# A decoder block on one core: three of four groups of gates computed behind the attention, in seven block products per pair

## The chip, the cores and the metric

The kernel is one launch on one core of a Trainium2 chip. The core has TensorE (PE, which has a separate track PEld for the loads of its stationary operand), VectorE (DVE), ScalarE (ACT), GpSimd (POOL) and SyncE (SP). Each engine works through its own list of instructions in order. SP does no arithmetic here: it starts the DMA transfers. The metric is the device time of one execution in microseconds (us).

## The reference

One layer of a decoder, in float32, for a sequence of 2048 rows of 1024 numbers. Cut to what matters:

```python
h = rmsnorm(x, attn_norm)
z = h @ w_in                       # pool channels | q | k | v | gate_pool | gate_attn
g_pool, g_attn = sigmoid(z[gate columns] + b_gate)          # 1024 columns each
a = pool_mixer(z[pool columns], w_pool, pool_scale)         # causal means over 2, 4, 8, 16 rows, minus the row
b = swa_sink_attention(q, k, v, sinks)                      # 16 query heads, window 128, blocks of 128
x = x + (g_pool * a + g_attn * b) @ w_out
h = rmsnorm(x, ffn_norm)
up = causal_depthwise_conv(h @ w_up, conv_w, conv_b)        # 2 x 2816 columns
x = x + (silu(gate) * val) @ w_down
```

The change is about the two gates: two matrices of 1024 x 1024 that multiply the same normalised input, whose results are scaled, put through a sigmoid, and multiplied with the pooled branch and the attention branch.

## The kernel before

**High and low parts.** TensorE is fed fp32r numbers. To keep float32 accuracy each operand is split into a high part (a cast, on ACT) and a low part (the source minus the high part, on DVE), and each product is three matmuls: high with high, high with low, low with high (`mm3`, L232). `split` (L213) makes the two parts of a raw weight tile: L221 is the cast, L222 the subtraction, each in two halves of 128x512.

**Chunks and projections.** The sequence is worked off in two chunks of 1024 rows. The hidden axis of 1024 is 8 tiles of 128 (k tiles). One projection of one slab of 128 output columns for half a chunk is 8 k tiles x 3 = 24 matmuls of 128x128 by 128x512; the kernel calls it a filler when it is placed between steps of the attention. The input `hs` is a list of 8 tiles, [128, 2 parts, 1024].

**The mixer** (L1422) is the part of a chunk that the change touches. First come keys and values of the chunk, then 32 attention items: four groups of query heads, 8 blocks each. An item is `scores` (L806: 8 matmuls of 128x256, then mask, maximum and four exponentials with their sums, L843), `probabilities` (L853: four transposes on PE L857, a cast on ACT L859, a subtraction on DVE L862 and a masking on POOL L865) and `values` (L874: four matmuls L885, then L895 on ACT and L896 on DVE). They are staggered: while item i has its scores, item i-1 has its transposes and item i-2 its values. Between them stand fillers, so that TensorE has work while ACT, DVE and POOL turn scores into probabilities.

**Which fillers.** `fillers(c, i)` (L143) deals out, for group i, the two gates of the slabs of group i-1 (`ga` for the attention, `gate_attn` L910, and `pg` for the pool, `gated` L954, with `combine` L966) and the pooled projection of group i (`pu`, `pooled` L921): 12 fillers over 8 items. Group 0 has queries in place of gates. The gates of group 3 (8 fillers) follow the last item, and the last item's `probabilities` and `values` run between them. Then `out_proj` (L994) multiplies the mixed tiles with w_out, `up` does w_up, and after it comes w_down.

**Seven block products.** The up projection already multiplies by a scheme with seven block products in place of eight: the class `Up` (L1111) takes a pair of weight slabs of 128 columns, splits both along the hidden axis, and the input in 2 x 2 blocks (hidden halves by halves of the chunk). Its methods `one` to `seven` are one block product each: `product` (L1098) issues 12 matmuls (4 k tiles x 3). The weights' sums A11, A12, A22, S1 to S4 are made by `Blocks` in four steps; the input's sums T1 to T4 are made by `right_t1` to `right_t4` and split by `parted` (L981: L984 on ACT, L985 on DVE).

**What sets the order of the weights.** `Stream` follows the list of `weight_order` (L155): it loads raw tiles into three buffers (pool `rp`, 4 KB per partition) up to three pieces ahead and splits them one or two ahead. Split weights go to the pool `up_` (19 buffers, 8 KB per partition), halves of a chunk to `fp` and `mp`. In chunk 0 the split weights of the mixer are also stored to HBM (`made`, `keep_weights` L247), and chunk 1 loads them back instead of splitting again. All DMAs are issued by SP in program order; each of them also waits until the one eight places before it has landed. A transfer that has to wait for a free buffer holds up those behind it on SP.

## Time and profile before

| | |
|---|---|
| Time, median of 3 runs | 2418.05 us (2417.07 to 2420.98) |
| The profiled execution's own time | 2418.99 us |
| Its span, first to last instruction | 2417.0 us |
| Granted TensorE clock | 0.999 |
| PE busy | 2397.2 us (99%), 11252 matmuls |
| DVE busy | 1838.6 us (76%) |
| ACT busy | 1122.9 us (46%) |
| POOL busy | 156.1 us (6%) |
| DMA queues | q1 (SP): 335.72 MB, 40.8% of 16 engines' span |

The page gives busy time per engine, the span in 40 slices, the DMA queues, the chain of work that ended last, and the costliest groups of instructions by line. The span of the profiled execution is 2.0 us shorter than its time, which lies around the span. In group rows, "mean" is the duration of one instruction; a matmul's mean (390 ns) contains the pipeline's depth, so the spacing of matmuls is read from runs of them in the timeline. The timeline gives start, duration, engine, line, tiles and count of each run of instructions, and in brackets the idle time before it with what ended it.

### The profile page before, as it was taken

The numbers are of one execution on the slowest core, as the hardware profiler recorded it, in microseconds if no ns is written. First come the engines' busy times: TensorE is split into PE (matmuls) and PEld (weight loads), VectorE is DVE, ScalarE is ACT, GpSimd is POOL, SyncE is SP. The second block draws the span as 40 slices with busy tenths as digits, with TensorE's granted clock in tenths as the row PEclk, the third lists the DMA queues.
The fourth block names the chain that finished last, engine by engine and source line by source line (L and its number), as shares of the span: only waits on it lengthen the run. The fifth ranks groups of instructions, "written<-read, shape, count | busy, mean of one in ns | idle before, by whom it ended". The sixth has DMA issues, their size and how long they took to land.

```text
span 2417.0 us, 30362 instructions
## 1 busy us (share of the span) xinstructions
PE 2397.2 (99%) x11252; PEld 1995.0 (83%) x11252; DVE 1838.6 (76%) x2966; ACT 1122.9 (46%) x2151; POOL 156.1 (6%) x102
## 2 busy tenths in 40 slices
PE   9999999999999999999999999999999999999999
PEld 8878888888888888788888888888888888888887
DVE  8687788765977777799946867765478777778994
ACT  7445444444555555543523533343446445554432
POOL 1113111000000000000002221110000000000000
PEclk9999999999999999999999999999999999999999
DMA  9755354268222233644344542231642222228421
GB/s 344 245 187 171 135 183 156 101 226 283 79 81 93 97 105 105 213 169 149 113 149 126 169 161 104 65 107 56 204 166 96 90 86 79 79 70 287 139 70 52
DMA packets 139026, 337.83 MB, mean 140 GB/s; under 512 B 12288, under 2 KB 48640, under 8 KB 127872
## 3 DMA queue, kind: packets, MB, share of 16 engines
q1 hardware_dynamic: 138448, 335.72, 40.8%
q8 instruction: 88, 1.44, 0.2%
q14 instruction: 58, 0.48, 0.1%
q10 hardware_dynamic: 432, 0.19, 0.0%
HBM read 231.67 MB, written 104.20 MB: 139 GB/s over the span
## 4 chain that ended last, share of the span: by engine, by line
PE 92%; DVE 3%; DMA 2%; ACT 2%; issue 1%; POOL 0%; SPq 0%; DVEq 0%; ACTq 0%; POOLq 0%
PE f L238 33%; PE f L1103 19%; PE t L1103 10%; PE a L1103 5%; PE f L1403 4%; PE a L1403 4%; PE s L1403 4%; PE t L1403 4%; PE a L885 2%; PE s L824 2%; PE a L238 1%; PE t L857 1%; DMA F<-xT 1%; DMA R<-w_out 0%; DVE U L222 0%
## 5 line engine op out<-in xcount | busy, mean ns | idle before, releaser
L238 PE MATMUL f<-U,U 128*128 128x512 f32 (+1 forms) x3936 | 917.0, 390 | 4.3 <-ACT U L221 1.8
L238 PEld LDWEIGHTS f<-U,U 128*128 128x128 f32 x3936 | 727.4, 188 | 154.7 <-DVE U L222 4.3
L1103 PE MATMUL f<-U,U 128*128 128x512 f32 x1512 | 359.8, 390 | 1.4 <-ACT Q L1121 1.4
L1103 PEld LDWEIGHTS f<-U,U 128*128 128x128 f32 x1512 | 283.4, 188 | 61.5 <-ACT Q L1121 2.2
L1169 DVE SCALAR_TENSOR_TENSOR M<-F,vc,M 128x1024 f32<-128x1024 f32 x176 | 225.3, 1282 | 140.9 <-ACT M L1166 140.5
L1103 PE MATMUL t<-U,U 128*128 128x512 f32 x1080 | 253.5, 389 | 0.8 <-ACT Q L1121 0.8
L1103 PEld LDWEIGHTS t<-U,U 128*128 128x128 f32 x1080 | 202.6, 188 | 43.2 <-ACT Q L1121 1.2
L843 ACT ACTIVATE Q<-s,st,rq 128x128 f32<-128x128 f32 x256 | 114.0, 455 | 106.6 <-DVE st L840 104.7
L334 ACT CAST U<-R 128x1024 fp32r<-128x1024 f32 x120 | 125.4, 1053 | 62.5 <-DVE R L363 31.1
L335 DVE TENSOR_TENSOR U<-R,U 128x1024 fp32r<-128x1024 f32 x120 | 146.5, 1222 | 0.0
L1103 PE MATMUL a<-U,U 128*128 128x512 f32 x576 | 139.3, 390 | 0.0
L1103 PEld LDWEIGHTS a<-U,U 128*128 128x128 f32 x576 | 108.0, 188 | 22.4
L865 POOL TENSOR_SCALAR_AFFINE_SELECT M<-M 128x1024 fp32r<-128x1024 f32 x64 | 90.8, 1419 | 541.9 <-DVE M L862 355.0
L1103 PE MATMUL f<-U,M 128*128 128x512 f32 x504 | 121.9, 389 | 0.3 <-DVE F L1147 0.3
L1361 ACT CAST U<-U 128x1024 fp32r<-128x1024 f32 x76 | 79.0, 1050 | 85.4 <-PE s L1403 22.9
L1103 PEld LDWEIGHTS f<-U,M 128*128 128x128 f32 x504 | 94.6, 188 | 20.3 <-DVE F L1147 0.7
L1166 ACT ACTIVATE M<-F,vc 128x1024 f32<-128x1024 f32 x88 | 109.4, 1243 | 2.0 <-DVE F L1151 0.5
L1155 ACT COPY F<-f 128x512 f32<-128x512 f32 x42 | 24.7, 589 | 175.4 <-PE f L1103 175.4
L222 DVE TENSOR_TENSOR U<-R,U 128x512 fp32r<-128x512 f32 x142 | 95.1, 700 | 8.0 <-ACT U L221 7.4
L1362 DVE TENSOR_TENSOR U<-U,U 128x1024 fp32r<-128x1024 f32 x76 | 92.1, 1220 | 4.1 <-ACT U L1361 3.9
L221 ACT CAST U<-R 128x512 fp32r<-128x512 f32 x142 | 80.7, 618 | 20.7 <-PE f L238 5.0
L1361 ACT CAST F<-U 128x1024 fp32r<-128x1024 f32 x44 | 46.2, 1050 | 92.7 <-PE a L1403 62.6
(271 smaller groups left out, 3569.9 us busy)
## 6 DMA issues: line engine op xcount, KB each, us to landing
R<-w_up SPq DMA_DIRECT2D x80, 512.0 KB, 3.8
actd<-M SPq DMA_DIRECT2D x44, 512.0 KB, 2.7
U<-w_down SPq DMA_DIRECT2D x88, 256.0 KB, 5.0
U<-actd SPq DMA_DIRECT2D x88, 256.0 KB, 5.3
qd<-U SPq DMA_DIRECT2D x64, 256.0 KB, 3.7
Q<-qd SPq DMA_DIRECT2D x64, 256.0 KB, 3.9
R<-w_out SPq DMA_DIRECT2D x32, 512.0 KB, 5.4
U<-kept SPq DMA_DIRECT2D x12, 1024.0 KB, 7.3
```

The source lines that it names most:

```text
L222: low = V.tensor_sub(lo[:, t], src[:, t], hi[:, t].bitcast(F32))
L238: nc.tensor.matmul(out, a, b, start=(i == 0), stop=(i == n - 1))
L334: A.copy(t[:, 0], raw)
L335: V.tensor_sub(t[:, 1], raw, t[:, 0].bitcast(F32))
L843: A.activation(pr[:, h, :], sc[:, h, 0:P], AF.Exp, bias=nm[:, h:h + 1], scale=it["rq"][:, h:h + 1], accum_out=rs[:, h:h + 1])
L865: G.affine_select(own.rearrange("p a h q -> p (a h) q"), pa.bitcast(F32).rearrange("p a h q -> p (a h) q"), pattern=[[0, 8], [1, P]], base ...
L1103: nc.tensor.matmul(bank, a[:, x, k, :], b[k // 2][:, y, k % 2, :], start=(first and i == 0), stop=(i == 11), skip_group_check=True)
L1166: A.activation(y, u[:, 2:], AF.Identity, bias=cw[:, 3, m:m + 1], scale=cw[:, 2, m:m + 1])
L1169: V.scalar_tensor_tensor(y, u[:, j:j + T], cw[:, j, m:m + 1], y, op0=ALU.mult, op1=ALU.add)
L1361: A.copy(hi, src)
L1362: V.tensor_sub(lo, src, hi.bitcast(F32))
L1403: nc.tensor.matmul(into[m], u[:, 0, c_], v[:, 1], start=(first and j == 0), stop=(k == n - 1 and j == 2), skip_group_check=True)
```

## The change

The eight items' fillers of each group are now one per item. Group 0 has the queries and pooled slabs that it had, group 1 queries, pooled slabs and the first gates of group 0, group 2 the next of them, and group 3 the last of them with its own pooled slab. So only the gates of group 0 (slabs 6 and 7) are still fillers. The gates of groups 1 to 3 are six units, one per slab (4, 5, 2, 3, 0, 1): the pair of w_ga and w_gp of that slab is multiplied with the input by the seven block products of the class `Up`, that is by 84 matmuls of 128x512 in place of 4 x 24 = 96. They run in `gates()` behind the attention; the first two block products of unit 0 (12 matmuls each) are the fillers of the last two items.

What goes with it:

- The input becomes 8 tiles of [128, 2 parts, 2 k tiles, 512] (`Input`), which serve as B11, B21 and B22. For T1 to T4 the chunk's x is read again from HBM (four transfers of 1 MB per chunk) and scaled on ACT (`scaled_input`, eight activations of 128x1024), and DVE subtracts.
- `split_added`: for `ga`, `pg`, `pu` and the first four `q` slabs in chunk 0, and for the units' weight blocks in both chunks, the low part is made without DVE. ACT casts the source to the high part (L235), ACT writes the negative of the source, cast, that is minus the high part, into the low part's place (L236), and an accumulating DMA from POOL's queue adds the source to it there (L237, 512 KB). There are 52 of these DMAs.
- The pooled difference d is stored to HBM (`dd`), as is the attention's output of groups 0 to 2 (`tad`), and the gated mix (`xd`); they are read back where they are needed. SP issues 839 DMAs in place of 757.
- The units' weights are not kept in `made`: chunk 1 loads the raw slabs and splits them again.
- The store of the carried keys and values moves ahead of the attention.

```diff
+UNITS = [ct for i in (1, 2, 3) for ct in slabs_of(i)]
+
+
 def fillers(c, i):
 
-    g = gates_of(i - 1) if i > 0 else queries_of(0) + queries_of(1)
-    pu = pooled_of(i)
-    if i == 0:
-        pu = pu[2:]
+    q = queries_of(0) + queries_of(1)
+    g = gates_of(0)
+    pu = [pooled_of(j) for j in range(4)]
+    if i == 3:
+        out = [[f] for f in g[6:] + pu[3] + [("one", 0, 0), ("two", 0, 0)]]
+        out[4].insert(0, ("gates", 0, 0))
+        return out
     fold = [("fold", j, 0) for j in FOLDS[FOLD_FIRST:] if c == 0 and i == 0]
-    out = fold + g[:4] + pu[:2] + g[4:] + pu[2:]
+    out = fold + (q[:4] + pu[0][2:] + q[4:6], q[6:] + pu[1][:2] + g[:2] + pu[1][2:],
+                  pu[2][:2] + g[2:6] + pu[2][2:])[i]
     return [out[n * len(out) // NB:(n + 1) * len(out) // NB] for n in range(NB)]
...
-        out += [(kind, j) for kind, j, n in gates_of(3) if n == 0]
+            out += [(kind, j) for parts in fillers(c, i) for kind, j, h in parts
+                    if h == 0 and kind not in ("one", "two")]
+        out += [("gates", i) for i in range(1, len(UNITS))]
...
+    def split_added(hi, lo, src):
+
+        A.copy(hi, src)
+        A.activation(lo, src, AF.Copy, scale=-1.0)
+        G.dma_start(lo, src.bitcast(F32R), accum_op=ALU.add)
...
+            if key[0] in ("ga", "pg", "pu") or key[0] == "q" and key[1] < 4:
+                split_added(hi, lo, raw)
+            else:
+                split_weights.last = split(hi, lo, raw)
...
-            A.copy(t[:, 0], raw)
-            V.tensor_sub(t[:, 1], raw, t[:, 0].bitcast(F32))
+            if self.added:
+                split_added(t[:, 0], t[:, 1], raw)
+            else:
+                A.copy(t[:, 0], raw)
+                V.tensor_sub(t[:, 1], raw, t[:, 0].bitcast(F32))
...
+    class Gates(Up):
+
+
+        def __init__(self, c, ct, b):
+            super().__init__(c, ct, b, None)
...
+    def scaled_input(c, j):
+
+        t = up_.tile([P, 2, T], F32, "U")
+        load(t, xT[2 * j * P:(2 * j + 2) * P, c * T:(c + 1) * T]
+             .rearrange("(k p) t -> p k t", p=P))
+        for k in range(2):
+            A.activation(t[:, k], t[:, k], AF.Identity,
+                         scale=vc[:, V_AN + 2 * j + k:V_AN + 2 * j + k + 1])
+        return t
+
+    def gates(c, units, b, xg, last_probabilities, last_values):
+
+
+        def weights(f, n):
+            if f < len(units):
+                if units[f].w is None:
+                    units[f].w = stream.get("gates", f)
+                units[f].w.step(n)
+
+        u0, u1, u2 = units[:3]
+        weights(1, 1)
+        u1.one()
+        last_probabilities()
+        weights(1, 1)
+        u1.two()
+        weights(2, 1)
+        right_t1(xg, b, None)
+        u2.one("t")
+        last_values()
+        xg += [scaled_input(c, j) for j in (2, 3)]
+        u2.two()
+        t2s = right_t2(xg, b, None)
+        u0.four()
+        right_t3(xg, b)
+        u0.three()
+        weights(1, 2)
+        u1.four("a")
+        u0.five()
+        right_t4(xg, b, t2s)
+        u0.fetch()
+        u0.six()
+        u0.seven()
+        u0.value()
+        weights(2, 1)
+        u1.three()
+        u0.gate()
+        weights(2, 2)
+        u1.five()
+        n = len(units)
+        for f in range(2, n):
+            u, old = units[f], units[f - 1]
+            if f > 2:
+                u.one()
+                u.two()
+            old.fetch()
+            weights(f + 1, 1)
+            old.seven()
+            old.value()
+            weights(f + 1, 1)
+            if f < n - 1:
+                u.three()
+            else:
+                u.four()
+            weights(f + 1, 1)
+            old.six()
+            old.gate()
+            weights(f + 1, 1)
+            if f < n - 1:
+                u.four()
+            else:
+                u.three()
+            u.five()
+        ms = {j: [mixed(j, 0)] for j in (3, 2, 1)}
+        x0 = up_.tile([P, 2, 2, 512], F32R, "U")
+        old.parts(x0)
+        stream.part(stream.used + 2)
+        u.fetch()
+        u.value(N1)
+        u.seven()
+        u.value(N0)
+        u.six()
+        u.attn()
+        for c_ in (N0, N1):
+            u.combine(c_)
+            if c_ == N0:
+                u.parts(x0)
+        ms[0] = [x0]
+        return ms
...
+            if units[0].w:
+                units[0].w.step(1)
+            if i == len(items) - 2:
+                run_later(9)
+                xg = [scaled_input(c, j) for j in (0, 1)]
+        done(items[-2])
         run_later(9)
-        if c + 1 < NCH:
-            for g in range(2):
-                load(carry[g, :, 0:2], kts[g][:, :, T - P:T].bitcast(F32))
-                load(carry[g, :, 2], vs[0][:, NB - 1, g].bitcast(F32))
-        for f in rest[2:4]:
-            filler(*f, c, hs, ta, st)
-            run_later()
-        ms = [mixed(ta, j) for j in (3, 2, 1)]
-        for f in rest[4:]:
-            filler(*f, c, hs, ta, st)
-            run_later()
-        stream.part(stream.used + 2)
-        return ms + [mixed(ta, 0)]
+        return gates(c, units, b, xg, lambda: probabilities(items[-1]), lambda: done(items[-1]))
```

How the order of instructions moves, at the end of the attention of chunk 0 (chunk 1 is alike). On PE, before, the rows from the last item's transposes (tile t) to its values (tile a), with a filler of 24 matmuls (tile f, weights U_350 to U_371 being the input's tiles in before) between them:

```order
L857 MATMUL t_4643<-identr_91,Q_4503 128x128 x4
L238 MATMUL f_4655<-U_350,U_4567 128x512 x3
L238 MATMUL f_4655<-U_353,U_4567 128x512 x3
L238 MATMUL f_4655<-U_356,U_4567 128x512 x3
L238 MATMUL f_4655<-U_359,U_4567 128x512 x3
L238 MATMUL f_4655<-U_362,U_4567 128x512 x3
L238 MATMUL f_4655<-U_365,U_4567 128x512 x3
L238 MATMUL f_4655<-U_368,U_4567 128x512 x3
L238 MATMUL f_4655<-U_371,U_4567 128x512 x3
L885 MATMUL a_4682<-M_4648,U_453 128x512 x2
L885 MATMUL a_4682<-M_4651,U_454 128x512 x2
L238 MATMUL f_4708<-U_350,U_4692 128x512 x3
```

In the change, the rows from unit 0's first block product (f_4046) on. The weights' tile U_3916 is unit 0's A11 and A12; U_4150 is unit 1's.

```order
L1161 MATMUL f_4046<-U_358,U_3916 128x512 x6
L924 MATMUL a_4096<-M_4036,U_452 128x512 x2
L924 MATMUL a_4096<-M_4039,U_453 128x512 x2
L863 MATMUL s_1581<-U_450,Q_3943 128x256 x8
L896 MATMUL t_4106<-identr_91,Q_4009 128x128 x4
L1161 MATMUL a_4116<-U_363,U_3916 128x512 x6
L1161 MATMUL a_4116<-U_368,U_3916 128x512 x6
L924 MATMUL a_4136<-M_4111,U_452 128x512 x2
L924 MATMUL a_4136<-M_4114,U_453 128x512 x2
L896 MATMUL t_4170<-identr_91,Q_4086 128x128 x4
L1161 MATMUL f_4155<-U_353,U_4150 128x512 x2
L1161 MATMUL a_4185<-U_363,U_4150 128x512 x2
```

Where 24 matmuls stood between two steps of the last items there are now 12, and from the last transposes (t_4170) on 2 of unit 1's first product and 2 of its second, whose other ten each follow the last values.

On ACT, in the change, the same place: L882 are the exponentials, L898 the cast behind the transposes, L934 the output's copies, L1179 the copy of unit 0's first product, L1386 the scaling of x, L235 and L236 the two steps of the split.

```order
L934 COPY Q_4024<-a_4019 64x256
L1179 COPY Q_4059<-f_4046 128x512
L1386 ACTIVATE U_4065<-U_4065,vc_127 128x1024
L934 COPY Q_4024<-a_4019 64x256
L1386 ACTIVATE U_4065<-U_4065,vc_127 128x1024
L1386 ACTIVATE U_4069<-U_4069,vc_127 128x1024 x2
L898 CAST M_4111<-t_4106 128x512
L882 ACTIVATE Q_4086,st_4082<-s_1581,st_4082,rq_207 128x128 x4
L885 ACTIVATE st_4082<-st_4082 128x4
L934 COPY Q_4101<-a_4096 64x256
L236 ACTIVATE U_4132<-R_3554 128x1024
L934 COPY Q_4101<-a_4096 64x256
```

Before, ACT had at this place only the attention's own rows (L843, L859, L895), the gates' L918 and L962, the casts of the mixed tiles L984, and halves of weights' casts L221:

```order
L895 COPY Q_4441<-a_4436 64x256 x2
L221 CAST U_4735<-R_4613 128x512 x2
L962 ACTIVATE F_4385<-f_4463,vc_127 128x512
L984 CAST U_4771<-U_1754 128x1024
L843 ACTIVATE Q_4503,st_4499<-s_1576,st_4499,rq_207 128x128 x4
L846 ACTIVATE st_4499<-st_4499 128x4
L895 COPY Q_4518<-a_4513 64x256 x2
L859 CAST M_4562<-t_4557 128x512
L984 CAST U_4774<-U_1754 128x1024
```

On POOL, in the change, the masking of items (L904) and the accumulating DMAs (L237) share one list; in before the list had only the masking here:

```order
L904 AFFINE_SELECT M_4039<-M_4036 128x1024
L904 AFFINE_SELECT M_4114<-M_4111 128x1024
L237 DMA U_4132<-R_3554 128x1024
L237 DMA U_4150<-R_3860 128x1024
L904 AFFINE_SELECT M_4178<-M_4175 128x1024
L237 DMA U_4203<-R_3882 128x1024
```

On SP, in the change, with the waits of each transfer (DMASW are accumulating DMAs, DMAHW transfers of SP's queue). R_34_3882 is the raw gate slab of unit 2, U_72 and U_73 the second half of x:

```order
L223 DMA U_66_4069<-xT 128x2x1024 [waits DMAHW5_49]
L223 DMA R_33_3862<-w_gp 128x1024 [waits DMASW1_49,DMAHW6_49,DVE_49,Activation_49]
L223 DMA dd_8_209<-F_43_4030 128x1024 [waits DMAHW7_49,DVE_49]
L223 DMA R_34_3882<-w_ga 128x1024 [waits DMASW2_49,DMAHW0_49,DMASW0_49,Activation_49]
L223 DMA U_72_4242<-xT 128x2x1024 [waits DMAHW1_49,PE_49]
L223 DMA U_73_4246<-xT 128x2x1024 [waits DMAHW2_49,PE_49]
```

The load of R_34 waits for an accumulating DMA, which frees its buffer, and the two loads of x stand behind it on SP; in before no transfer of SP waited for POOL's queue.

More of the change, by code (lines that the diff above doesn't have):

```diff
@@ L975, in filler @@
             fold(j)
+        elif kind == "gates":
+            a[-1]["units"][j].w = stream.get("gates", j)
+        elif kind in ("one", "two"):
+            getattr(a[-1]["units"][j], kind)()
         else:
```

119 lines of the change are left out of this document (88 added, 31 removed).

## The prediction

> **What bounds the kernel now.** First the page's totals and its chain of work that ended last:
>
> ```profile
> span 2417.0 us, 30362 instructions
> PE 2397.2 (99%) x11252; PEld 1995.0 (83%) x11252; DVE 1838.6 (76%) x2966; ACT 1122.9 (46%) x2151; POOL 156.1 (6%) x102
> ...
> PE 92%; DVE 3%; DMA 2%; ACT 2%; issue 1%; POOL 0%; SPq 0%; DVEq 0%; ACTq 0%; POOLq 0%
> ```
>
> TensorE is busy 2397.2 of 2417.0 us, so all the others are hidden, and matmuls that go save their time only if nothing takes TensorE's place. Next the timeline of PE, first inside the attention (L824 scores, L885 values, L857 transposes, L238 projections), then where it ends:
>
> ```profile
> 243.56 1.11 PE L824 MATMUL s<-U,Q 128*128 128x256 f32 x8
> 244.51 1.09 PE L885 MATMUL a<-M,U 128*128 128x512 f32 x4
> 245.44 0.60 PE L857 MATMUL t<-identr,Q 128*128 128x128 f32 x4
> 245.80 5.72 PE L238 MATMUL f<-U,U 128*128 128x512 f32 x24
> 251.36 1.11 PE L824 MATMUL s<-U,Q 128*128 128x256 f32 x8
> ...
> 459.39 0.60 PE L857 MATMUL t<-identr,Q 128*128 128x128 f32 x4
> 459.74 5.72 PE L238 MATMUL f<-U,U 128*128 128x512 f32 x24
> 465.30 1.07 PE L885 MATMUL a<-M,U 128*128 128x512 f32 x4
> 466.20 71.33 PE L238 MATMUL f<-U,U 128*128 128x512 f32 x314
> 537.78 5.91 PE L238 MATMUL f<-U,U 128*128 128x512 f32 x24 [0.25 <-DVE U L222]
> ```
>
> No row up to 537.78 has idle time in brackets: the last item, the gates behind it and the start of the output projection are seamless. 314 matmuls took 71.33 us, 0.227 us each. By the starts of the rows, scores are 0.95 us, values 0.93, transposes 0.36, a filler 5.5. So an item with one filler lasts 7.8 us, which is what every item of the change gets. The attention lives on the cover of its fillers: between the last transposes (459.39) and the values that need them (465.30) stand 5.5 us of matmuls, while ACT, DVE and POOL make the masked probabilities.
>
> **What is removed.** Six pairs of slabs with 84 in place of 96 matmuls are 72 per chunk, 144 in all: 144 x 0.227 = 32.7 us. This is the gain, and nothing on PE is added. DVE loses the subtractions of weights and of the attention's fillers; it is at 76% and not the bound, so this is worth nothing by itself.
>
> **Attention with one filler per item.** Such items occur already, in group 0 of both chunks, with small waits like these:
>
> ```profile
> 1321.07 1.22 PE L824 MATMUL s<-U,Q 128*128 128x256 f32 x8 [0.36 <-ACT Q L843]
> 1322.59 0.63 PE L857 MATMUL t<-identr,Q 128*128 128x128 f32 x4 [0.30 <-DVE Q L849]
> ```
>
> The row at 251.36 shows that 7.8 us is enough in steady state. I take 2 us in all for chunk 0, where low parts now come by DMA while the first weights are still arriving, and 0 for chunk 1 (bounds 0 and 6). The seam to the output projection, where the last unit's mix is made in front of it, gets 0.5 (0 to 3).
>
> **The end of the attention.** Here the change puts 12 matmuls (2.7 us) where 24 stood, and between the last transposes and the values only four (0.9 us). The durations of what must fit in between:
>
> ```profile
> L334 ACT CAST U<-R 128x1024 fp32r<-128x1024 f32 x120 | 125.4, 1053 | 62.5 <-DVE R L363 31.1 <-DVE R L355 29.7 <-issue 0.5
> L843 ACT ACTIVATE Q<-s,st,rq 128x128 f32<-128x128 f32 x256 | 114.0, 455 | 106.6 <-DVE st L840 104.7 <-issue 1.8
> L895 ACT COPY Q<-a 64x256 f32<-64x256 f32 x128 | 47.1, 368 | 53.9 <-DVE U L896 52.0
> L859 ACT CAST M<-t 128x512 fp32r<-128x512 f32 x64 | 37.6, 588 | 93.0 <-PE t L857 92.8
> L846 ACT ACTIVATE st<-st 128x4 f32<-128x4 f32 x64 | 13.3, 208 | 5.9 <-DVE st L845 5.9
> L613 ACT ACTIVATE F<-F 128x1024 f32<-128x1024 f32 x8 | 8.5, 1063 | 0.0
> ...
> L862 DVE TENSOR_TENSOR M<-t,M 128x512 fp32r<-128x512 f32 x64 | 43.9, 686 | 2.0 <-ACT M L859 0.7
> ...
> L865 POOL TENSOR_SCALAR_AFFINE_SELECT M<-M 128x1024 fp32r<-128x1024 f32 x64 | 90.8, 1419 | 541.9 <-DVE M L862 355.0 <-DVE st L845 174.7 <-DVE F L950 12.3
> ```
>
> and, from the timeline, the first and the last of one item's four exponentials:
>
> ```profile
> 444.64 0.46 ACT L843 ACTIVATE Q<-s,st,rq 128x128 f32<-128x128 f32 x1 [2.00 <-DVE st L840]
> ...
> 446.31 0.20 ACT L843 ACTIVATION_READ_ACCUMULATOR Q<-s,st,rq 128x1 f32 x1
> ```
>
> They last from 444.64 to 446.51, 1.9 us. I count from the start of unit 0's first block product, in ACT's new order (activations of 128x1024 at 1.05): cast of transposes 0.6, high part of unit 0's next block 1.05, exponentials 1.9 and their small follower 0.2, copy 0.4, copy of the block product 0.6, then the four scalings of x with a copy between, 4.2 + 0.4, cast 0.6, the last item's exponentials 1.9 + 0.2, copy 0.4, minus-high part of unit 0's block 1.05: **13.4**. Its accumulating DMA can leave now. A copy, unit 1's high part, a copy, unit 1's minus part: **16.3**, and unit 1's DMA can leave. A copy and the cast behind the last transposes: 17.2. Then DVE's subtraction 0.7 and POOL's masking 1.4, with the hops 19.4, and the last values end at **20.3**. TensorE's own work up to there is 2.7 + 0.9 + 0.95 + 0.4 + 2.7 + 0.9 + 0.4 + 0.9 + 0.9 = 10.9. So it loses 9.4 us per chunk with no DMA counted: ACT, 46% busy on the whole, has 17 us of work in a stretch in which TensorE has 11. Before, no scaling and no split of 128x1024 stood among these rows, and no wait.
>
> **The low parts by DMA.** Let X be the time of one accumulating DMA of 512 KB, L that of a raw load. Behind the last values TensorE takes the rest of unit 1's first two products, which need the low part: 16.3 + X. Unit 2 is a longer chain. Its raw buffer is free when unit 0's DMA has landed, 13.4 + 0.3 + X; then the load L, two activations 2.1, and its own DMA X: 15.8 + 2X + L. TensorE's work up to there is 10.9 + 4.5 (twenty matmuls) + 1.6 (seven) = 17.0. No accumulating DMA is in the trace. The nearest rows:
>
> ```profile
> R<-w_up SPq DMA_DIRECT2D x80, 512.0 KB, 3.8
> actd<-M SPq DMA_DIRECT2D x44, 512.0 KB, 2.7
> ...
> R<-w_out SPq DMA_DIRECT2D x32, 512.0 KB, 5.4
> U<-kept SPq DMA_DIRECT2D x12, 1024.0 KB, 7.3
> ```
>
> L is 3.8 to 5.4, middle 4.6. X lies between the 512 KB store, 2.7, and 7.3, a transfer of twice the bytes, since it reads two tiles and writes one. I take 4.6, the middle of the two loads. Then unit 2's low part is there at 15.8 + 9.2 + 4.6 = 29.6, and TensorE is 29.6 - 17.0 = 12.6 us behind; that contains the 9.4.
>
> The Trainium skill ("DMA: Bandwidth & Descriptors", section "Anatomy of one DMA — SWDGE (gpsimd) path") fits a DMA from POOL's queue as about 2.0 us plus its bytes at 436 GB/s. For 512 KB that is an estimate of 3.2 us, and by it unit 2 would be 9.8 us behind. No run here shows one yet, and whether the fit holds for an accumulating transfer the page does not say.
>
> **Behind that**, the second half of x is queued on SP behind unit 2's raw load: issued at 18.3, with the 7.3 of a 1 MB row at 25.6 and a little later for the second, then scaled (2.1 each pair), subtracted, cast and subtracted again for T2 (1.2 + 1.05 + 1.2 for each half): I get it some 3 us late. The next three blocks' low parts each wait for a freed raw buffer and a DMA; 3 us at this X. Tail 6.0 (bounds 0, if the lateness of TensorE gives all of it time, and 11 at X = 7.3). From unit 3 on a block has 14 us or more of matmuls between its minus part and its first use, so nothing there waits at X = 4.6.
>
> **Sum.** Loss per chunk 12.6 + 6.0 = 18.6. From the profiled execution's 2418.99 (0.04% above the median): 2418.99 - 32.7 + 37.2 + 2.0 + 0.5 = **2426.0**. With X = 2.7, L = 3.8 the ACT chain alone decides, 9.4, and the tail shrinks to 4.4: 2418.99 - 32.7 + 27.6 + 2.5 = 2416.4. With X = 7.3, L = 5.4: unit 2 at 35.8, 18.8 behind, tail 11: 2418.99 - 32.7 + 59.6 + 2.5 = 2448.4.
>
> **Rivals.**
>
> *The ramp costs only ACT's chain.* If the DMAs land in about 3 us and TensorE, late anyway, gives the x chain and the next blocks their time, 9.4 per chunk is all: 2418.99 - 32.7 + 18.8 + 2.5 = 2407.6, faster. It decides wherever 15.8 + 2X + L is below 17.0 + 9.4, so X under 3.4 with L = 3.8, and the second half of x is ready by TensorE's 36. For it: the 2.7 us row, and the page's row of DMA shares, where the slice of the last items (423 to 483 us, the eighth digit) has 2:
>
> ```profile
> DMA  9755354268222233644344542231642222228421
> ```
>
>  Against: two 512 KB loads at 3.8 and 5.4. If even the chain is partly covered, it goes towards 2395.
>
> *The low parts land in 2.7 to 3.2, the tail stays.* 2416.4 at 2.7. By the skill's 3.2 us, with 9.8 and a tail of 4.4: 2418.99 - 32.7 + 28.4 + 2.5 = 2417.2. Either is no change.
>
> *The three raw buffers throttle the units.* A buffer is free when the DMA that reads it has landed; load, two casts, two blocks' splits and X make a cycle of L + 0.6 + 1.4 + 2.1 + 1.4 + 2.1 + X = 16.8 at 4.6 and 4.6, against a unit's 84 x 0.227 = 19.1 us. With X = 7.3, L = 5.4 it is 20.3: 1.2 more for about eight units, 9.6 on top of 2448.4, so 2458. It decides from X + L of 11.5. For it: 1 MB takes 7.3. Against: the store of 512 KB takes 2.7, and X and L would both have to be at their upper ends.
>
> **How the numbers follow.** The forecast has a chance of 0.45 (its own range 2419 to 2446), ACT's chain alone 0.30, the short DMAs with the tail 0.15, the throttle 0.10. What can be told from no change begins at 0.2%, 4.8 us, so at 2413.2 and 2422.9. All of the second case but for a tenth of it, and a little of the third, are faster: 0.32. The rest of these two and a small part of the forecast are the same: 0.18. Slower: 0.50. The range leaves out the throttle and the lowest of the fast case: 2400 to 2446.
>
> **What would show it.** Right: PE idle in front of the last transposes and values, released by ACT's exponentials and by POOL's mask; idle in front of unit 1's and unit 2's products, released by a DMA of POOL's queue; a loss of about 19 us in the first 50 us behind the attention, in both chunks alike; L1386 rows ahead of the last exponentials. Wrong: a landing time of POOL's DMAs far from 4.6; idle in later units or in the attention's groups 1 to 3; the four scalings of x somewhere else in time than in front of the exponentials, because x landed late, which would make the first number larger.

## The result and the profile after

The change takes 2498.3 us (median, 2497.6 to 2499.9) against 2418.4 us of the kernel before, measured with it: ratio 1.033, with a 95% interval of 1.031 to 1.035. It is 80 us slower; 2426 was predicted, with a range of 2400 to 2446.

The page of the changed kernel, totals and chain:

```profile
span 2496.9 us, 30624 instructions
PE 2403.2 (96%) x11108; PEld 1977.8 (79%) x11108; DVE 1898.7 (76%) x2994; ACT 1254.9 (50%) x2279; POOL 204.1 (8%) x154
...
PE 78%; DVE 7%; DMA 6%; ACT 4%; issue 4%; POOL 0%; SPq 0%; DVEq 0%; ACTq 0%; POOLq 0%
```

144 matmuls are gone (11252 to 11108), yet PE's busy time has risen from 2397.2 to 2403.2 us. Part of it is the pipeline that runs empty ahead of each wait: a matmul of 128x512 alone lasts 0.39 us, in a run one starts every 0.227, so each of the 71 waits in brackets (24 before) adds some 0.16 us of busy time. The larger part is that many matmuls run slower; the granted clock of the span is 0.989 in place of 0.999. The chain of waits says the same in other words: PE has 78% of it in place of 92%, and DVE, DMA, ACT and issue have taken the difference.

To see where, I went through the timeline of PE and took, for each run of matmuls, the time from its start to the start of the next, less its count times the spacing that undisturbed runs show (0.227 us for 128x512, 0.119 for 128x256, 0.088 for 128x128). What is left over is lost time: waits, and matmuls that ran slower. "First scores" means the first of 128x256; one item with scores of 128x128 stands about 9 us ahead of them. Summed by stage, in us:

| Stage | before | change |
|---|---|---|
| start to the first scores of chunk 0 | 13.6 | 21.3 |
| attention, chunk 0 (to unit 0's first product; before: to the last transposes) | 9.0 | 23.4 |
| end of attention, units 0 to 2, chunk 0 (before: last gates) | 0.1 | 26.9 |
| units 3 to 5, chunk 0 | | 15.2 |
| output projection, chunk 0 | 4.8 | 10.5 |
| up and down of chunk 0, start of chunk 1 | 5.7 | 5.4 |
| attention, chunk 1 | 5.9 | 7.4 |
| end of attention, units 0 to 2, chunk 1 (before: last gates) | -0.3 | 25.6 |
| units 3 to 5, chunk 1 | | 14.7 |
| the rest | 1.3 | 3.8 |
| sum | 40.1 | 154.2 |

The difference is 114.1; less the 32.7 that the removed matmuls save, 81.4, and the spans differ by 79.9. Of the 154.2 us, 86 are idle time that the timeline shows in brackets (13.7 before); the other 68 (26 before) are matmuls at less than full speed, the 0.16 us ahead of each bracket, and gaps too short for a bracket.

The timeline of PE where the attention of chunk 0 ends, from unit 0's first product on:

```profile
385.45 3.00 PE L1161 MATMUL f<-U,U 128*128 128x512 f32 x12
...
391.09 0.73 PE L924 MATMUL a<-M,U 128*128 128x512 f32 x2 [1.67 <-POOL M L904]
...
394.24 0.63 PE L896 MATMUL t<-identr,Q 128*128 128x128 f32 x4 [1.47 <-DVE Q L888]
...
400.06 1.20 PE L924 MATMUL a<-M,U 128*128 128x512 f32 x4 [2.36 <-DVE F L1191]
...
407.00 1.22 PE L924 MATMUL a<-M,U 128*128 128x512 f32 x2 [1.05 <-POOL M L904]
410.20 3.91 PE L1161 MATMUL f<-U,U 128*128 128x512 f32 x10 [1.99 <-DMA U<-R]
413.95 2.45 PE L1161 MATMUL a<-U,U 128*128 128x512 f32 x10
...
419.95 2.56 PE L1161 MATMUL t<-U,U 128*128 128x512 f32 x10 [1.75 <-DMA U<-R]
...
429.21 0.50 PE L1161 MATMUL f<-U,U 128*128 128x512 f32 x1 [2.39 <-ACT U L1036]
429.69 3.85 PE L1161 MATMUL t<-U,U 128*128 128x512 f32 x9
```

Before, this place was one run of 314 matmuls. Now nearly every step waits: for the mask (POOL L904), for the normalised exponentials (DVE L888), for low parts by DMA (U<-R), for T2's cast (ACT L1036). And ten matmuls from 410.20 to 413.95 took 0.375 us each on average, where the next ten took 0.23. The clock that the throttle granted, in the table by windows (the number ahead of the DMA share), shows why:

```profile
400.00:405.00 5.00, 3.27 (x13) 1.87 (x13) 3.17 (x8) 4.88 (x8) 2.25 (x3) 1.00 0.48 93
405.00:410.00 5.00, 1.95 (x4) 0.69 (x3) 2.45 (x3) 0.19 (x1) 1.48 (x1) 0.63 0.99 223
410.00:415.00 5.00, 4.80 (x15) 3.86 (x16) 1.29 (x2) 2.86 (x4) 0.87 (x1) 0.69 0.95 363
```

PE was busy 5.2 of the 10 us from 400 to 410. Four windows of 2.5 us from 405 on have a clock of 0.75, 0.50, 0.50 and 0.88, which is half speed for about 6.8 us; in it the matmuls start 0.427 us apart, behind it 0.227. The Trainium skill's page "TensorE: Matmul & The Clock Gate" (section "Part 1: The HAM clock gate") says that an idle window of about 3.4 us halves the clock and a busy one gives it back. The trace agrees in the two speeds, and the length is that of two such windows. But no single wait of TensorE at this place was longer than 2.4 us: several waits close together were enough.

Where units 4 and 5 of chunk 0 run, the timeline of PE, then ACT's and SP's:

```profile
509.02 7.17 PE L1161 MATMUL f<-U,U 128*128 128x512 f32 x24 [3.61 <-ACT Q L1179]
...
527.66 7.59 PE L1161 MATMUL t<-U,U 128*128 128x512 f32 x22 [4.31 <-DMA U<-R]
```

```profile
501.75 1.14 ACT L229 CAST U<-R 128x512 fp32r<-128x512 f32 x2 [9.31 <-DMA R<-w_out]
...
508.40 0.57 ACT L1179 COPY Q<-f 128x512 f32<-128x512 f32 x1
```

```profile
493.02 0.33 SPq L223 DMA_DIRECT2D R<-w_gp  x1
496.00 0.33 SPq L223 DMA_DIRECT2D R<-w_out  x1
```

ACT stood 9.3 us at the head of its list for a raw slab of w_out, whose load SP could start only at 496.00, behind the last gate slab's. The copy that frees unit 5's PSUM bank (L1179) is queued behind that cast, and PE waited for the copy.

The wait at 527.66 is for unit 5's last low part. What stood ahead of it, in the timelines of POOL and DVE:

```profile
505.98 0.88 POOL L237 DMA_DIRECT2D U<-R  x1 [14.88 <-DVE R L377]
...
519.41 0.89 POOL L237 DMA_DIRECT2D U<-R  x1 [7.29 <-DVE M L1365]
```

```profile
511.15 0.69 DVE L384 TENSOR_TENSOR R<-R,R 128x512 f32<-128x512 f32 x1 [3.84 <-DMA U<-R]
```

The sums S1 and S4 (L384, L385) are written over the raw gate slab. So the accumulating DMA of A11 and A12, which reads that slab (505.98), has to land first, at 511.03. Then come the sums, ACT's two steps and the unit's last DMA (519.41), which lands after 8.20 us. TensorE had come to that product at 523.35.

### The profile page after: what moved, and what is told of

The parts are those of the page before. It is cut to its first block, busy times and chain, and to the rows that moved or that the text cites. A ratio compares the mean times of both kernels' runs of the same rounds, so it can differ in the third digit from the quotient of the medians.

```text
span 2496.9 us, 30624 instructions
## 1 busy us (share of the span) xinstructions
PE 2403.2 (96%) x11108; PEld 1977.8 (79%) x11108; DVE 1898.7 (76%) x2994; ACT 1254.9 (50%) x2279; POOL 204.1 (8%) x154
## 4 chain that ended last, share of the span: by engine, by line
PE 78%; DVE 7%; DMA 6%; ACT 4%; issue 4%; POOL 0%; SPq 0%; DVEq 0%; ACTq 0%; POOLq 0%
PE f L1161 20%; PE f L252 18%; PE t L1161 12%; PE a L1161 6%; PE f L1593 4%; PE a L1593 4%; PE s L1593 4%; PE t L1593 4%; DMA U<-R 2%; PE a L924 1%; PE s L863 1%; PE a L252 1%; ACT Q L882 1%; PE t L896 1%; DMA R<-w_gp 1%
## 5 line engine op out<-in xcount | busy, mean ns | idle before, releaser
L252 PE MATMUL f<-U,U 128*128 128x512 f32 (+1 forms) x2784 | 652.3, 390 | 13.7 <-ACT U L229 5.4
L252 PEld LDWEIGHTS f<-U,U 128*128 128x128 f32 x2784 | 511.0, 189 | 122.8 <-ACT U L229 7.2
L1161 PE MATMUL f<-U,U 128*128 128x512 f32 x1872 | 456.6, 395 | 18.1 <-ACT Q L1179 9.0
L1161 PEld LDWEIGHTS f<-U,U 128*128 128x128 f32 x1872 | 354.7, 191 | 101.0 <-ACT Q L1179 13.8
L1161 PE MATMUL t<-U,U 128*128 128x512 f32 x1392 | 339.4, 397 | 16.2 <-DMA U<-R 13.8
L1161 PEld LDWEIGHTS t<-U,U 128*128 128x128 f32 x1392 | 265.2, 191 | 77.0 <-DMA U<-R 16.3
L1161 PE MATMUL a<-U,U 128*128 128x512 f32 x768 | 187.3, 390 | 2.9 <-DMA U<-R 2.9
L1161 PEld LDWEIGHTS a<-U,U 128*128 128x128 f32 x768 | 143.7, 188 | 33.6 <-DMA U<-R 3.7
L1161 PE MATMUL f<-U,M 128*128 128x512 f32 x624 | 151.5, 390 | 2.1 <-DVE F L1205 2.1
L882 ACT ACTIVATE Q<-s,st,rq 128x128 f32<-128x128 f32 x256 | 114.0, 455 | 60.8 <-DVE st L879 58.6
L904 POOL TENSOR_SCALAR_AFFINE_SELECT M<-M 128x1024 fp32r<-128x1024 f32 x64 | 93.6, 1463 | 334.3 <-DVE st L884 205.5
L1179 ACT COPY Q<-f 128x512 f32<-128x512 f32 x104 | 61.0, 586 | 51.0 <-PE f L1161 50.9
L924 PE MATMUL a<-M,U 128*128 128x512 f32 x240 | 73.2, 411 | 13.4 <-POOL M L904 5.3
```

The source lines that it names most:

```text
L252: nc.tensor.matmul(out, a, b, start=(i == 0), stop=(i == n - 1))
L882: A.activation(pr[:, h, :], sc[:, h, 0:P], AF.Exp, bias=nm[:, h:h + 1], scale=it["rq"][:, h:h + 1], accum_out=rs[:, h:h + 1])
L904: G.affine_select(own.rearrange("p a h q -> p (a h) q"), pa.bitcast(F32).rearrange("p a h q -> p (a h) q"), pattern=[[0, 8], [1, P]], base ...
L924: nc.tensor.matmul(pv, v, p[:, a], start=(i == 0), stop=(i == 2 * len(todo) - 1))
L1161: nc.tensor.matmul(bank, a[:, x, k, :], b[k // 2][:, y, k % 2, :], start=(first and i == 0), stop=(i == 11), skip_group_check=True)
```

## The experiments

**Who makes the low parts.** The first kernel is the change with its low parts by DVE:

```diff
     def split_added(hi, lo, src):
         A.copy(hi, src)
-        A.activation(lo, src, AF.Copy, scale=-1.0)
-        G.dma_start(lo, src.bitcast(F32R), accum_op=ALU.add)
+        V.tensor_sub(lo, src, hi.bitcast(F32))
```

> The change, with every low part that it makes by ACT and an accumulating DMA made by ACT and DVE instead (cast 128x1024, subtraction 128x1024), in the attention's fillers and in the units. Theory: the low parts by DMA carry the losses of the attention of chunk 0 (14 us more than before), of the units (15 us per chunk), of the seam to the output projection (6) and about half of the ramp (13 of 26 per chunk): 2498 - 14 - 30 - 6 - 26 = 2422, between 2410 and 2440. Rival: one filler per item and three raw buffers cause them, whoever makes the low part: 2485 or more. A second rival: DVE, at 76%, becomes late with 52 subtractions of 1.2 us more: waits of TensorE for DVE in the units, 2450 or more.

The second does so in the units alone:

```diff
-            return Blocks(raws, key[0] == "gates")
+            return Blocks(raws)
```

> The change, with low parts by DVE in the units' weight blocks alone; the attention's fillers keep the accumulating DMA. Theory: 2498 - 30 (units) - 26 (ramp) - 6 (seam) = 2436, the attention of chunk 0 keeps its 14 us. Rival (whoever makes the low part, the raw ring throttles): 2490 or more. The difference to the kernel with all low parts by DVE is what the DMA costs in the attention: 14 by the theory, 0 by the rival that one filler per item costs it.

Measured: 2446.4 and 2446.7 us (ratios to before 1.011 and 1.012, 1.009 to 1.015), above the first theory's 2440. So making the units' low parts by an accumulating DMA costs 52 us, and in the attention nothing more than DVE would. The lost time by stage, with low parts by DVE everywhere: attention of chunk 0 to its last scores 27.3 (the change 26.0), then to the end of the output projection 22.9 (51.3); in chunk 1 10.5 (9.4) and 13.6 (40.6). From unit 0's first product through unit 2 the loss falls from 26.9 to 14.9 in chunk 0 and from 25.6 to 13.3 in chunk 1, in units 3 to 5 from 15 to 0.6 in both. The theory was right for these two places. It was wrong for the attention, where 14 us were expected back and none came, and for the output projection of chunk 0, where 6 were expected back: it loses about 11 us either way. The rival that the attention's loss comes with one filler per item, whoever makes the low part, stands for that part. Nor did DVE become the bound in the units: of PE's waits between 421 and 540 us one is left in brackets, 0.31.

The reverse, the kernel before with low parts by DMA in its fillers:

```diff
-            split_weights.last = split(hi, lo, raw)
+            if key[0] in ("ga", "pg", "pu") or key[0] == "q" and key[1] < 4:
+                split_added(hi, lo, raw)
+            else:
+                split_weights.last = split(hi, lo, raw)
```

> The kernel before, with the low parts of the gates, the pooled slabs and the first four query slabs of chunk 0 by ACT and the accumulating DMA, as in the change; no units, no other edit. If the DMA's time alone makes the attention of chunk 0 slow: 2418 + 10 to 14 = 2430, all of it between 130 and 460 us. If it needs one filler per item to show (less cover, buffers turned over sooner): 2418 to 2422.

Measured: 2441.9 us, ratio 1.0095 (1.007 to 1.013): 22.4 us more, where the theory allowed 10 to 14. All of it lies in the attention of chunk 0, where lost time goes from 8.8 to 33.4. PE's waits, and the time from issue to landing of the 28 DMAs:

```profile
PE f L244 <- DMA U<-R: 5.7, 4, 2.4
PE s L833 <- ACT Q L852: 5.0, 5, 2.5
PE a L894 <- POOL M L874: 3.6, 3, 1.3
PE a L894 <- ACT M L868: 3.2, 3, 1.1
...
DMA to landing us min/median/max: 4.5/7.1/13.6
```

So even with two fillers in some items the DMA's time is not hidden here: 5.7 us are waits for it directly. The others are waits for ACT, which has a second activation per low part in this kernel, and for POOL, which issues the DMAs in the list that holds the masks; how much of them follows from the DMA's time is not shown. Over before's 9, the attention of chunk 0 loses 25 us more with these DMAs alone, 18 more with one filler per item and no DMA, and 17 more in the change, which has both: they don't add up.

**How many fillers an item has.** This kernel has low parts by DVE and the two edits told of further down, and block products for four units per chunk instead of six, so that ten fillers stand in eight items, and the last item has 24 matmuls:

```diff
-UNITS = [ct for i in (1, 2, 3) for ct in slabs_of(i)]
+UNITS = [ct for i in (2, 3) for ct in slabs_of(i)]
...
+    out = (fold + q[:4] + pu[0][2:] + q[4:], g[:4] + pu[1][:2] + g[4:6] + pu[1][2:],
+           g[6:] + pu[2][:2] + g1[:4] + pu[2][2:], g1[4:] + pu[3] + [("one", 0, 0), ("two", 0, 0)])[i]
```

> As the kernel with the late scaling, but with block products for groups 2 and 3 alone (four units per chunk); the gates of group 1 are fillers again, so groups 0 to 3 have 10 fillers for 8 items, and the last item's filler is unit 0's first two products together, 24 matmuls. It has 48 matmuls more than the change: +10.9 us. Theory (one filler per item leaves ACT, DVE and POOL too little time in chunk 0, 17 us of loss there; the last items want a full filler): the attention of chunk 0 falls back by 10 or more, the ramps by 3 each: 2432 + 11 - 16 = 2427. If the density of fillers does not matter: 2443.

Measured: 2438.7 us, ratio 1.008 (1.005 to 1.011), against 2442.2 with one filler per item and else the same edits. The lost time of chunk 0's attention falls from 28.2 to 11.4, of chunk 1's from 10.6 to 7.4; the matmuls that are back cost 10.9. So with low parts by DVE the attention of chunk 0 hangs on the number of fillers per item. The ramps, put at 3 us less each, did not follow: from the last scores to the end of the output projection chunk 0 loses 23.7 in place of 19.2, chunk 1 11.4 in place of 12.4. The 2427 also stood on a kernel with the late scaling at 2432, which came out at 2442. The loss in the attention does not come from DVE's load as a sum. In the tables by windows, the attention with low parts by DVE and six units, and with four:

```profile
141.00:392.00 251.00, 236.01 (x1187) 193.71 (x1187) 216.92 (x451) 131.43 (x405) 53.86 (x32) 0.99 0.52 174
```

```profile
140.00:417.00 277.00, 272.20 (x1368) 227.30 (x1367) 236.88 (x473) 138.96 (x413) 54.97 (x32) 1.00 0.53 181
```

DVE is busy 86% of both (216.9 of 251, 236.9 of 277). What differs is the time from an item's scores to its transposes and on to its values that TensorE has covered. One place shows how little it takes, POOL's timeline in the kernel with all low parts by DVE:

```profile
207.36 5.43 POOL L823 TENSOR_TENSOR rq<-rq,mhalf 128x32 f32<-128x32 f32 x1 [7.36 <-DVE st L878]
212.75 1.10 POOL L903 TENSOR_SCALAR_AFFINE_SELECT M<-M 128x1024 fp32r<-128x1024 f32 x1
```

An item's mask (L903) stands behind the queries' 5.4 us power (L823) on POOL, and PE waits 3.97 us for it. Before has the same pair under two fillers, and its values at 201.66 don't wait. PE in the kernel with low parts by DVE, then POOL and PE in before:

```profile
213.90 1.22 PE L923 MATMUL a<-M,U 128*128 128x512 f32 x2 [3.97 <-POOL M L903]
```

```profile
195.79 5.43 POOL L785 TENSOR_TENSOR rq<-rq,mhalf 128x32 f32<-128x32 f32 x1 [9.49 <-DVE rq L782]
201.18 1.10 POOL L865 TENSOR_SCALAR_AFFINE_SELECT M<-M 128x1024 fp32r<-128x1024 f32 x1
```

```profile
201.66 1.40 PE L885 MATMUL a<-M,U 128*128 128x512 f32 x4
```

Why chunk 1 loses so much less with one filler per item (4 us more than before, at the same 85% of DVE) I have not separated: it has no weights to split, no DMA for them and fewer stores, all at once.

**The start.** Three kernels ask why the first scores of chunk 0 come late, in before and in the change:

```profile
133.62 1.22 PE L824 MATMUL s<-U,Q 128*128 128x256 f32 x8 [0.53 <-ACT Q L843]
```

```profile
141.40 1.22 PE L863 MATMUL s<-U,Q 128*128 128x256 f32 x8 [0.51 <-ACT Q L882]
```

The change with its input tiles all taken at the first step:

```diff
-                h = hs.at(k, 0) if n == 1 else hs.fresh(k, n // 2)
+                if n == 0 and k % 2 == 0:
+                    hs.fresh(k, 0)
+                    hs.fresh(k, 1)
+                h = hs.at(k, n // 2)
```

> The change, with the eight pair tiles of the input of chunk 0 all taken from the pool at the first of the three steps that fill them, as before did with its eight tiles; nothing else. Theory: the 7.7 us that the first scores come later (141.4 in place of 133.6) are the wait of the second half's casts for buffers of the pool, which they get late: 2490.5, first scores at 134. Rival: the start is late for another reason (order of transfers, low parts): 2498.

Measured: 2499.0 us, first scores at 142.3. When the tiles are taken makes no difference. Next, the kernel with low parts by DVE, with the casts of the input's second half one step earlier:

```diff
-            if c == 0 and n == 3:
+            if c == 0 and n == 2:
                 make_h(0, 2, hs)
```

> The change with all low parts by DVE (2446.4), and the second half of chunk 0's input cast one step of the key loop earlier in the program (at n = 2 in place of n = 3), which puts the eight casts at rows 56 to 59 of ACT's list in place of 101 to 111; before has them at 62 to 89. Theory: the 7.7 us that the first scores come late are these casts' place in ACT's order: 2446.4 - 7.7 = 2439, first scores at 134. Rival: the start is late because of something else in the pair tiles: 2446.

Measured: 2445.1 us, first scores at 139.2. The waits for these casts are gone, and a new one of 3.5 us for DVE stands at 48.86, where the casts now crowd the keys' own work. The first scores gain 2.0 us, a quarter of what was expected. Then the kernel before with nothing but the pair tiles (the class `Input` of the change, and the places that read it):

```diff
-            if n == 0:
-                hs.append(up_.tile([P, 2, T], F32R, "U"))
+                h = hs.at(k, 0) if n == 1 else hs.fresh(k, n // 2)
...
-        mm3(out, [(w[:, 0, k, :], w[:, 1, k, :], hs[k][:, 0, c], hs[k][:, 1, c])
+        mm3(out, [(w[:, 0, k, :], w[:, 1, k, :], hs.at(k, n)[:, 0], hs.at(k, n)[:, 1])
...
-    hs, kvw, raws = [], [], []
+    hs, kvw, raws = Input(), [], []
```

> The kernel before with one edit: the input's eight tiles of 128x2x1024 become the change's eight pair tiles of 128x2x2x512, the second half's taken from the pool when they are filled. If the pair tiles alone make the start late: 2418 + 6 to 8 = 2425, first scores at 140. If the start is late in the change because of something else (other program order behind it, stores): 2418 to 2420, first scores at 134.

Measured: 2426.2 us against 2418.7, ratio 1.0033 (1.002 to 1.004). This is the whole 7.5 us, first scores at 141.86. ACT's timeline, with the casts of the second half (L227):

```profile
65.78 1.33 ACT L227 ACTIVATE U<-U,vc 128x512 fp32r<-128x512 f32 x2 [0.94 <-PE f L238]
```

They begin at 65.8, and PE waits for them four times, 2.6 us in all. In before one of the eight ran at 34.7 and seven between 41 and 49 us, among other work, four of them here:

```profile
42.80 2.56 ACT L227 ACTIVATE U<-U,vc 128x512 fp32r<-128x512 f32 x4
```

So it is shown that the pair tiles alone make the start late. That they do it by the place of these casts in ACT's list is not shown: the kernel with the casts one step earlier had them between 40.7 and 45.7 and gained a quarter. Ahead of the casts TensorE waits in the kernel with pair tiles 1.13 us for ACT at 57.86 and 1.94 us for DVE at 60.53, and for 5 us from 60 on its granted clock is 0.50. Why the lists come out otherwise with these tiles is not settled.

**The scaling of x.** The kernel with the earlier casts, and the first four scalings moved behind the last exponentials:

```diff
         weights(2, 1)
+        for j in (0, 1):
+            scale_input(xg[j], j)
         right_t1(xg, b, None)
```

> As the kernel with the second half early, and the first four scalings of x moved in the program from the last item but one to in front of T1's subtractions, so behind the last exponentials. Theory (ACT's list is what makes the end of the attention late): 4.2 us of ACT work leave the chain to the last values, 3 to 4 us per chunk less: 2439 - 7 = 2432. Rival (T1 and T2 come later by the same time and the wait moves to u0's S products): no gain, 2437 to 2440.

Measured: 2442.2 us, 2.9 less than without, whose two runs are 2.2 apart. Lost time falls 0.7 in chunk 0 and 2.5 in chunk 1 at this place. The theory expected 7, so most of the 4.2 us of ACT that leave the chain are taken up by what comes next.

**The raw buffers.** The change itself, with low parts by DMA:

```diff
-    rp = pool("rp", 3)
-    up_ = pool("up", 19)
+    rp = pool("rp", 5)
+    up_ = pool("up", 18)
```

> The change itself (low parts by DMA), with five raw buffers in place of three, and 18 split buffers in place of 19. If the units (15 us per chunk behind the first 80 us) wait because a raw buffer is held until its accumulating DMA has landed: the units' waits go, 2498 - 25 = 2473 or less. If they wait for the landing of their own low parts, however early they are loaded: 2490 to 2500. One split buffer less may cost a few us elsewhere.

Measured: 2492.7 us, ratio 1.030 (1.027 to 1.033). The time alone lies in the range of the second expectation, but part of it is lost elsewhere. The start and the attention of chunk 0 lose 12 us more, which the split buffer given up may explain; from the last scores to the end of the output projection it loses 10 less in chunk 0 and 7 in chunk 1. Units 3 to 5 still lose 12 and 9 us of their 15. PE's wait for ACT's copy at the head of unit 5 is 0.74 us in place of 3.61, while waits for the low parts themselves remain:

```profile
522.19 2.56 PE L1161 MATMUL f<-U,U 128*128 128x512 f32 x10 [3.18 <-DMA U<-R]
...
534.36 6.71 PE L1161 MATMUL t<-U,U 128*128 128x512 f32 x22 [3.72 <-DMA U<-R]
```

In front of the second wait stands the same chain as in the change: the DMA of A11 and A12 at 517.56, 4.58 us, then the sums over the gate slab and ACT's two steps, then the last DMA at 526.03, 8.29 us. So both are at work: the buffers held until the DMA has landed, and the DMA's own time, which a unit meets twice in a row because its sums are written over the raw slab. No kernel here kept the sums out of the raw slabs, so the two are not priced apart. More buffers mend about a third of what DVE's subtractions mend.

**The clock.** The change with 32 matmuls more per chunk, which multiply the input with itself; nobody reads them:

```diff
+        def busy(n):
+            hot = ps2.tile([P, T], F32, "s")
+            x = b["B11"][0]
+            for i in range(n):
+                nc.tensor.matmul(hot[:, 0:512], x[:, 0, 0, 0:P], x[:, 0, 0, :], start=True, stop=True)
...
         weights(2, 1)
+        busy(12)
...
+        busy(8)
         u2.two()
...
         right_t3(xg, b)
+        busy(12)
         u0.three()
```

> The change itself, with 32 extra matmuls of 128x512 per chunk behind the attention (12, 8 and 12) whose result nobody reads; they stand in slots where TensorE waits. Theory (after some us with much idle time the granted clock falls, PEclk 0.63 to 0.69 in the stretches around 410 and 432 us, and the matmuls that follow take 0.375 us in place of 0.227): the extra work goes into idle time and the slow stretches go, PEclk 1.00 between 400 and 440 us, and the time falls by 3 to 8 us though 64 matmuls (14.5 us) are added: 2490 to 2495. Rival (the slow matmuls wait for something else, such as their operands): the time rises by the part of the 14.5 us that finds no idle slot, 2500 to 2512, and matmuls of 0.375 us remain.

Measured: 2502.0 us, 3.7 more, though 14.5 us of matmuls are added. This is in the rival's range, and the theory's gain did not come. From 400 to 410 us the granted clock is 1.00 (before that edit 0.81), from 420 to 430 it is 0.89, behind a longer wait for the next low part:

```profile
400.00:410.00 10.00, 8.41 (x36) 6.12 (x37) 6.23 (x12) 4.41 (x8) 3.25 (x3) 1.00 0.79 181
...
420.00:430.00 10.00, 10.00 (x41) 8.15 (x40) 4.88 (x6) 6.91 (x9) 0.00 (x0) 0.89 0.32 103
```

```profile
418.95 4.05 PE L1161 MATMUL t<-U,U 128*128 128x512 f32 x10 [3.06 <-DMA U<-R]
```

The slow stretch at 406 is gone. But one as long stands ahead of the extra matmuls, where the change has none: from 391 to 398 us the clock is 0.53 (1.00 in the change), and unit 0's second product takes 4.73 us in place of 3.00:

```profile
394.54 4.73 PE L1161 MATMUL a<-U,U 128*128 128x512 f32 x12
```

Over the whole span the clock is 0.989, as in the change. So the slow stretches have moved and not gone, and what they cost by themselves is not shown. Where the clock did come back, between 400 and 410, little was gained by it: what the faster matmuls win they lose at the next DMA, and unit 2's product starts at 418.95 in place of 419.95. About three quarters of the extra matmuls cost no time, since TensorE waits there anyway.

No version here beats the kernel before. The best of the change's kind, four units with low parts by DVE, is 0.8% slower than it.

## Why the prediction was wrong, point by point

The sum came out 72 us short. Units 3 to 5 are 29.9 of it, the end of the attention 15.3, the attention of chunk 0 12.4, the start 7.7 and the output projection of chunk 0 5.2.

**The gain** of 32.7 us is there: 144 matmuls fewer, and the up and down stages are unchanged in their losses.

**The end of the attention** was forecast by its mechanism, and rightly, but sized low. Counted from unit 0's first product (385.45), the minus part of unit 0's next block was ready at 15.4 (13.4 predicted), that of unit 1 at 18.2 (16.3), the last values ended at 22.8 (20.3), unit 2's low part was there at 34.5 (29.6). Two of its steps were too short. ACT was still 1.2 us in an earlier split when I started its count, and the DMAs took 4.6 and 6.0 and the load 5.5, where 4.6 was taken for all three. The chain of waits for this place:

```profile
401.26 4.58 DMA U<-R
...
405.98 5.48 DMA R<-w_ga
...
413.89 6.02 DMA U<-R
```

In the prediction's own terms TensorE was 34.5 - 17.0 = 17.5 us behind at unit 2's product (12.6 predicted) and lost 9.4 more behind it (6.0 predicted): 26.9 in chunk 0 and 25.6 in chunk 1, in place of 18.6. With low parts by DVE, so without a DMA in the chain, 14.9 and 13.3 are lost, where the prediction had 9.4 for ACT's chain alone. (TensorE's own work up to the last values adds up to 10.75, not 10.9, and ACT's first count to 13.5, not 13.4; neither matters here.)

The brackets hold 17.5 and 16.3 us of these losses. The other 9.4 and 9.3 the sum left out: about 6.4 are matmuls that run slower behind such waits, and the rest is the 0.16 to 0.2 us ahead of each of 14 brackets. The kernel before had it in its trace, where 57 matmuls behind a wait took 15.2 us in place of 12.9; I passed that row by:

```profile
557.17 15.16 PE L238 MATMUL f<-U,U 128*128 128x512 f32 x57 [1.77 <-ACT U L221]
```

The prediction named only the work that DVE loses. On the whole DVE gained: it is busy 1898.7 us in place of 1838.6. No term of the sum hung on that.

**X** was taken as 4.6. All 52 DMAs:

```profile
U<-R POOLq DMA_DIRECT2D x52, 512.0 KB, 5.4
...
DMA to landing us min/median/max: 4.5/5.4/11.8
```

The range of 2.7 to 7.3 held the median, not the spread: in the attention of chunk 0 the median was 8.1 between 100 and 300 us. The estimate of 3.2 us from the Trainium skill's fit ("DMA: Bandwidth & Descriptors", "Anatomy of one DMA — SWDGE (gpsimd) path") is below the shortest of them, so for an accumulating transfer between tiles of SBUF the measurement decides against it.

**Units 3 to 5** were put at nothing: "a block has 14 us or more of matmuls between its minus part and its first use, so nothing there waits". They lost 15 us per chunk. This step failed most. It took the minus part for early, and it came late: unit 5's last one was ready at 519.0, and TensorE came to its product at 523.35, 4.3 us later and not 14. What makes it late stands ahead of it: the raw slab that an earlier DMA of the same unit still reads while the sums wait to be written over it, the next load that waits for such a buffer, and the output projection's casts that wait for that load at the head of ACT's list. The rival of the throttle had the buffers right and priced them at 9.6 us altogether, by a cycle time of 20.3 against 19.1. That is a mean; the waits came at the end of the units, where w_out's slabs join the same three buffers, and it had no term for the sums. With DVE's subtractions 0.6 of the 15 us are left, with five buffers 12 and 9: the buffers alone are the smaller part.

**Attention with one filler per item** was put at 2 us for chunk 0 and cost 14.4. I read "7.8 us is enough" off a place of before where single fillers alternate with double ones, and took it for a whole chunk. For chunk 1 the estimate of 0 was near (1.5). The attribution that I made next, to the DMA, fell too.

**The start** was not in the sum at all. The edit of the input's tiles looked like a change of shape, at no cost. With it eight casts on ACT come 25 to 31 us later, other waits appear ahead of them, and the first scores come 7.7 us later; which of the two does it is open.

**The output projection** of chunk 0 lost 5.7 more (0.5 predicted). The accumulating DMA is not the cause, since it loses as much with low parts by DVE. The reloads of the mixed tiles join stores that already fill the queues there (a DMA share of 0.87 before the change, between 507 and 592 us); that this is the reason was not tested.

**The rivals**: that the ramp costs ACT's chain alone, 0.30, and that the DMAs are short, 0.15, were both wrong in the same direction. All cases priced the places that I had found and none left room for ones that I had not, and the range with them.

## What to carry to other kernels

Where TensorE is 99% busy, its fillers are cover for other engines' chains, and work that is removed there must be priced with the cover that goes: count, for each chain, the time between its two ends on TensorE, before and after. A transfer that writes a low part also holds its source, so look at who waits for that buffer, to load it or to write over it, down to the stage that follows. And a wait of TensorE costs more than its length when several stand close together, unless the next step is late anyway.

## What the runs showed of the hardware that I had not expected

An accumulating DMA of 512 KB between two SBUF tiles takes 4.5 us at least and 5.4 in the median, 7.1 to 8.1 in the attention of chunk 0, where other transfers run; POOL is held 0.87 us by each issue. TensorE's granted clock was halved for 6.8 us behind several waits of 2.4 us and less, and while it was down a matmul of 128x512 took 0.427 us in place of 0.227. And the input in tiles of another shape, with nothing else changed, made the whole kernel 7.5 us slower.
